# Attention logits as 64-row products on the two halves of the array

## The chip, the core and the metric

The kernel runs on one core of one Trainium2 chip. The core has TensorE (PE), which multiplies matrices; VectorE (DVE), ScalarE (ACT) and GpSimd (POOL), which work on vectors; SyncE (SP), which here only issues transfers; and 16 DMA engines that move data between HBM and SBUF, the on-chip memory of 128 partitions. PE writes its results into PSUM, a second memory of eight banks, and the other engines read them there. The metric is the time in microseconds of one execution on the device.

## What is computed

The reference is one layer of an encoder, applied to two requests with the same weights: a prompt of 1024 tokens (A in the kernel) and a sample of 512 tokens (B). After a normalisation one wide projection gives the columns of two branches. Branch A of the layer is a bidirectional mLSTM; branch B is a dilated window attention with three groups (window and dilation 128 and 1, 512 and 4, 2048 and 16) of 8 heads of 64 channels. The change touches only the attention, and of it only the logits:

```python
logits = jnp.einsum('bghnqe,bghnke->bghnqk', qr, kb) + bias[:, None]
logits = jnp.where(mask, logits, -jnp.inf)
mx = jnp.max(logits, axis=-1)
p = jnp.exp(logits - mx[..., None])
den = jnp.sum(p, axis=-1)
o = jnp.einsum('bghnqk,bghnke->bghnqe', p, vb)
```

The contraction of a logit runs over the 64 channels (e) of one head. The three groups are then mixed by their denominators, gated, projected, merged with the other branch and added to the input.

## The kernel before

Precise products of 32-bit numbers are made from two parts: each operand is split into a high and a low part in the type float32r, and three products (high by high, high by low, low by high) are added in one PSUM bank. The helper `mm3` (lines 211 to 213) is such a triple for the dense projections.

The program has stages. The prompt's long projections come first, then the mLSTM of A (`mlstm`), the attention of A (`attend`, `N.attend(A, ...)`), the mLSTM of B, the attention of B, and the last projections. From the first mLSTM on, the order of PE and of the SP queue is written out by hand (`manual_schedule`), and the order on DVE, ACT and POOL is a scheduler's. In the hand-written order a stage's own work alternates with steps of dense work of the same layer (`Fill`; a step is one `mm3` triple or so), a fixed number of steps for each stage (`STEPS`).

The attention works on pairs of heads. There are 12 units `u` for a request, group `g` and pair `pr` (`g, pr = divmod(u, 4)`), and each has `T.n` tiles of 128 queries: 8 for A, 4 for B, so 96 + 48 = 144 tiles. A tile is wide when the residue sub-sequence `S // dil` is longer than 128 (groups 0 and 1 of A, group 0 of B: 64 + 16 = 80 tiles) and reads 256 keys; the other 64 tiles are narrow and read 128 keys. For a tile there are four steps, in `stages`: `products` (the logits into the bank `lg`), `softmax` (DVE adds the bias and takes the maximum, line 1386, then ACT takes the exponential, line 1390), `turn` (PE transposes the weights into `pt`, line 1397, and ACT or DVE copies them out, lines 1400 and 1402) and `output` (PE multiplies by the values into `o`, lines 1411 and 1418, and ACT copies, lines 1414 and 1420). `att_round` runs one round for each tile: `products` of this tile, `softmax` of the one before, `turn` of the one before that, a helping of dense steps (`fill(1)`), and then `output` of the tile three rounds back. So on PE a round reads: `lg`, `pt`, dense, `o`, and the next round's `lg` follows directly on `o`.

How `products` uses the array differs between the two kinds of tile. Queries and keys lie in HBM in `T.aqk`, 128 rows for a pair: 64 channels of the first head, then 64 of the second, once for the high and once for the low part.

- Wide: the query operand of one head holds its high part in 64 rows and its low part in the other 64; the key operand of that head holds the same part of the keys twice, in both halves. One product with the high keys and one with the low keys, each over all 128 rows, then give all four combinations: 2 products for a head, 4 for a tile, each of 256 columns (line 1372).
- Narrow: the key operand is block diagonal: 128 columns with the first head's rows and zeros below, then 128 columns with zeros above and the second head's rows. One `mm3` of 128 rows and 256 columns serves both heads: 3 products for a tile. The zeros are set by memsets on POOL (line 1312), once for each buffer.

`att_load` queues the transfers for these layouts; `tick` issues some of the queue (SP) in each round. For a wide unit they are 4 for the queries and 8 for the keys, of 64 rows each, and for a narrow unit 1 and 4.

The tiles of PSUM in the attention are `lg`, `pt` and `o`, two buffers each, six banks together; two more are the dense projections'.

Of the kernel before, what the change touches and what calls it, by code (L numbers as in the profile page):

```python
# [22 lines left out]
F32 = mybir.dt.float32  # L23
# [6 lines left out]
P = 128  # L30
D = 1024
KT = D // P
BLK = 512
# [150 lines left out]
class Net:  # L184
    def __init__(self, tc, a):
        self.tc, self.nc, self.a = tc, tc.nc, a
        self.clock = self.lag = 0
        self.pending, self.owner = [], {}
        self.defer, self.mixed, self.rows = False, set(), {}
        self.queued, self.pace = [], 1  # L190
        self.side = self.nc.sync
        self.lows = None
        self.scans, self.state, self.held, self.sum = [], [], [], None
        self.low_part = None
        self.retired = []
        self.narrow, self.acc, self.direct = {}, [None, None], {}


    def pool(self, stack, name, bufs, side, space=None):
# [1068 lines left out]
    def att_load(self, T, u):  # L1268

        nc = self.nc
        g, pr = divmod(u, 4)
        S, n, dil = T.S, T.n, min(DILS[g], T.n)
        wide = S // dil > P
        A, B = slice(0, 64), slice(64, P)
        half = lambda x, i: x[:, i % 2 * 2 * S:(i % 2 + 1) * 2 * S]  # L1280
        if S == BLK:
            if u == 0:
                self.qs, self.avs = self.take("Q0"), self.take("X1", F32)
            q, v = half(self.qs, u), half(self.avs, u // 2)
            keys = lambda: [x for z in [self.take(f"V{u % 2}a")] for x in (z[:, :2 * S], z[:, 2 * S:])]
        else:
            if pr % 2 == 0:
                self.avs = self.take(f"K{u // 2 % 2}", F32)
            q, v = self.take(f"Q{u % 2}"), self.avs
            keys = lambda: [self.take(f"V{u % 2}{x}") for x in "ab"]  # L1290
        q = q.rearrange("p (a s) -> p a s", a=2)
        v = v.rearrange("p (n c) -> p n c", c=256)
        qd, kd = T.aqk[:, u], T.aqk[:, u + 12]
        if wide:
            kk = [x.rearrange("p (h s) -> p h s", h=2) for x in keys()]
            for hh, rows in enumerate((A, B)):
                self.queue(("att", u), ("aqk", S, u), q[rows, hh].bitcast(F32), qd[0, rows])
                self.queue(("att", u), ("aqk", S, u), q[(B, A)[hh], hh].bitcast(F32), qd[1, rows])
                for to in (A, B):
                    for i in range(2):  # L1300
                        self.queue(("att", u), ("aqk", S, u + 12), kk[i][to, hh].bitcast(F32), kd[i, rows])
            k = [x[:, hh] for x in kk for hh in range(2)]
        else:
            new = (T, u % 2) not in self.narrow
            if new:
                self.narrow[T, u % 2] = [x.rearrange("p (n b s) -> p n b s", n=n, b=2) for x in keys()]
            k = self.narrow[T, u % 2]
            self.queue(("att", u), ("aqk", S, u), q.bitcast(F32), qd.rearrange("a p s -> p a s"))
            for side, rows in enumerate((A, B)):
                for i in range(2):  # L1310
                    if new:
                        nc.gpsimd.memset(k[i][rows, :, 1 - side].bitcast(F32), 0.0)
                    self.queue(("att", u), ("aqk", S, u + 12), k[i][rows, :, side].bitcast(F32), kd[i, rows].rearrange("p (n s) -> p n s", s=P))
        if pr % 2 == 0:
            c0 = 512 * g + 256 * (pr // 2)
            x = S // dil // P
            for r in range(dil):
                self.queue(("att", u), ("av", S), v[:, r * x:(r + 1) * x],
                           T.av[:, c0:c0 + 256].rearrange("(x p r) c -> r p x c", p=P, r=dil)[r])
        return [q[:, 0], q[:, 1]], k, v  # L1320

    def attention(self, T, u, qkv, bias, sb, ps):

        nc = self.nc
# [3 lines left out]
        wide = L > P  # L1328
# [30 lines left out]
        def stages(turned, qp, kp, kt, bt, dst, ends):  # L1359
# [4 lines left out]
            ts = {}  # L1364

            def products():
                lg = self.bank("lg")
                if wide:
                    ts["lg"] = [lg[:, 0], lg[:, 1]]
                    for hh in range(2):  # L1370
                        for z in (k[hh], k[2 + hh]):
                            nc.tensor.matmul(lg[:, hh], q[hh][:, qs], z.rearrange("p (n j) -> p n j", j=P)[:, pair],  # L1372
                                             start=z is k[hh], stop=z is not k[hh])
                else:
                    kk = [z[:, kt[0]].rearrange("p a j -> p (a j)") for z in k]
                    ts["lg"] = [lg[:, 0, :P], lg[:, 0, P:2 * P]]
                    self.mm3(lg[:, 0], (q[0][:, qs], q[1][:, qs]), kk, True, True)

            def softmax():
                ls = ts["ls"] = sb.tile([P, 2, W], F32, name="ls", bufs=3)  # L1380
# [48 lines left out]
    def attend(self, T, fill, steps, first, banks, outs, after=None, beside=None, at=()):  # L1429

        nc = self.nc
        self.lag = 3
        with ExitStack() as st:
            ps = self.pool(st, "at_ps" + T.name, 2, "right", PSUM)
            sb = self.pool(st, "at" + T.name, 2, "right")
            shape = {"lg": [P, 2, 256], "pt": [P, 4, P], "o": [P, 4, P]}
            make = lambda b: ps.tile(shape[b], F32, name=b, bufs=2)
            spare = {b: make(b) for b in banks}  # L1440
            self.bank = lambda b: spare.pop(b) if b in spare else make(b)
            self.ot = Rot(self, [sb.tile([P, OW], F32, name=f"ot{i}", bufs=1) for i in range(outs)])
            tables = self.pool(st, "bias" + T.name, 1, "right")
            bias = Rot(self, [tables.tile([P, BLK], F32, name=f"bias{i}", bufs=1) for i in range(4)])
            if T.n > 4:
                tables.tile([P, 2560], F32, name="apart", bufs=1)
            tiles = []
            fill.stage(steps, 12 * T.n)

            self.xo_end = fill.done + steps  # L1450

            def ready(u):
                nonlocal bias
                if u == 4 and T.n <= 4:
                    b = [x[F32] for x in bias.bufs]
                    bias = Rot(self, [b[i][:, c:c + 256].bitcast(F32R) for i in range(2) for c in (0, 256)])
                    self.xo_bufs.insert(0, ("stage", b[2:]))
                return self.attention(T, u, first if u == 0 else self.att_load(T, u), bias, sb, ps)

            coming = ready(0)  # L1460
            self.need(("table", 0))
            for i in range(12):
                now = coming
                for j, t in enumerate(now):
                    if j == 1:
                        if i < 11:
# [304 lines left out]
def body(tc, a):  # L1771
# [3 lines left out]
    with ExitStack() as st:  # L1775
# [145 lines left out]
        with ExitStack() as s1:  # L1921
# [35 lines left out]
            with ExitStack() as s2:  # L1957
# [11 lines left out]
                with ExitStack() as s3:  # L1969
                    N.gate_sums(B, N.pool(s3, "sums", 1, "right"))  # L1970
                    lanes = N.lanes(B, N.pool(s3, "lane2", 1, "right"), lambda: N.bank("o").rearrange("p a b -> p (a b)"), True)
                    N.attend(A, fill, STEPS[1], kept["qkv"], ("pt", "o", "lg"), 10, hold("head", lambda: N.ml_load(B, 0)),
                             lanes, range(44, 96, 8))
                    for _ in lanes:
                        pass
                    N.close()
# [16 lines left out]
            N.rows_in = [N.sraw[:, :BLK]] + [N.osb.tile([P, BLK], F32, name=f"ymr{i}") for i in range(2)]  # L1993
            N.xo_bufs = [(i, [N.osb.tile([P, BLK], F32, name=f"xo{i}{j}") for j in range(2)]) for i in range(2)]
            N.postw = None
            N.attend(B, fill, STEPS[3], kept["qkv"], ("lg", "o", "pt"), 7)
# [70 lines left out]
```

## Time and profile before

| | |
|---|---|
| median of 3 runs | 2236.23 us (2234.92 to 2236.70) |
| profiled execution | 2236.86 us, of which the span of the trace is 2235.1 us |
| PE, PE's weight loads, DVE, ACT, POOL busy | 99%, 87%, 68%, 50%, 32% of the span |
| attention of A | about 1310 to 1618 us after the start of the span |
| attention of B | about 1835 to 2088 us |

How it is read: each instruction on PE that multiplies has a load of its weights ahead of it (PEld in the trace), which may run beside the product before it. The duration of a product counts from when it is taken up until its result is complete, so the durations of successive products overlap; what a product costs in a full stream is the distance between its start and the next one's start. A row such as `128*128 128x256` reads: weights of 128 rows by 128 columns, a moving operand of 128 rows by 256 columns. A product of 32-bit type (the `o` of line 1418 and 1411) stands as two records.

### The profile page before, as it was taken

Reading aid. Unit: us, or ns where it says so; the run is one execution under the profiler, and the core shown is the slowest. Engines: PE = TensorE matmul, PEld = TensorE weight load, DVE = VectorE, ACT = ScalarE, POOL = GpSimd, SP = SyncE. Lnnn points to the kernel's source line nnn. Section 1 sums busy time; section 2 is a strip of 40 time slices with the busy share of each in tenths; the row PEclk is TensorE's granted clock in tenths of the full one; section 3 lists DMA queues with packets and bytes.
Section 4 is the critical chain, followed back from the end, with each engine's and each line's share of the span. In section 5 each row is a group of like instructions: output and inputs, shape, how many; then the busy total and the mean of one; then the engine's idle time right before and its main releaser. Section 6 shows DMA issues by size and latency. Waiting matters only on the chain.

```text
span 2235.1 us, 34988 instructions
## 1 busy us (share of the span) xinstructions
PE 2218.1 (99%) x11962; PEld 1939.6 (87%) x11962; DVE 1523.7 (68%) x2989; ACT 1120.3 (50%) x2394; POOL 715.7 (32%) x988
## 2 busy tenths in 40 slices
PE   9999999999999999999999999999999999999998
PEld 8999888888888888888888889989888888888887
DVE  7775667687776665558887765555689855665674
ACT  7332343344444343456776655656666644554332
POOL 1000423333333222236677620011165522221221
PEclk9999999999999999999999999999999999999999
DMA  3742444433323223385754779997678887776663
GB/s 124 192 115 81 174 155 165 165 141 113 113 105 112 85 85 122 114 279 173 236 186 157 191 200 247 260 250 210 208 242 289 259 261 236 236 255 201 232 233 113
DMA packets 217661, 408.81 MB, mean 183 GB/s; under 512 B 24938, under 2 KB 128042, under 8 KB 217483
## 3 DMA queue, kind: packets, MB, share of 16 engines
q1 hardware_dynamic: 187784, 298.51, 42.7%
q0 software_dynamic: 26096, 95.47, 13.7%
q10 hardware_dynamic: 3602, 12.59, 1.4%
q8 instruction: 95, 1.56, 0.3%
q14 instruction: 84, 0.68, 0.1%
HBM read 286.75 MB, written 119.73 MB: 182 GB/s over the span
## 4 chain that ended last, share of the span: by engine, by line
PE 94%; issue 2%; DMA 2%; DVE 1%; ACT 1%; POOL 0%; SPq 0%; DVEq 0%; POOLq 0%; ACTq 0%
PE d L213 14%; PE d L211 14%; PE d L212 14%; PE dense L211 12%; PE dense L213 12%; PE dense L212 12%; PE o L1418 3%; PE pt L1397 2%; PE lg L1372 2%; PE num L213 1%; PE num L211 1%; PE num L212 1%; PE a L1088 1%; PE kv L211 1%; PE kv L212 1%
## 5 line engine op out<-in xcount | busy, mean ns | idle before, releaser
L211 PE MATMUL dense<-H,wh 128*128 128x512 f32 x664 | 270.3, 407 | 0.0
L213 PE MATMUL dense<-H,wl 128*128 128x512 f32 x664 | 260.6, 392 | 0.0
L212 PE MATMUL dense<-H,wh 128*128 128x512 f32 x664 | 260.4, 392 | 0.0
L212 PE MATMUL d<-Hl,phla 128*128 128x512 f32 x608 | 236.5, 389 | 0.0
L213 PE MATMUL d<-Hh,phla 128*128 128x512 f32 x608 | 236.5, 389 | 0.0
L211 PE MATMUL d<-Hh,phla 128*128 128x512 f32 x608 | 236.5, 389 | 0.0
L280 DVE TENSOR_TENSOR wl<-wraw,wh 128x1024 fp32r<-128x1024 f32 (+1 forms) x121 | 150.0, 1240 | 72.8 <-ACT wh L274 72.5
L1386 DVE CUSTOM_DVE_ANT_0 ls<-lg,bias 128x256 f32<-128x256 f32 (+2 forms) x336 | 103.0, 332 | 116.5 <-PE lg L1372 55.4
L211 PE MATMUL d<-Hh,phlb 128*128 128x512 f32 x456 | 177.4, 389 | 0.0
L212 PE MATMUL d<-Hl,phlb 128*128 128x512 f32 x456 | 177.4, 389 | 0.0
L213 PE MATMUL d<-Hh,phlb 128*128 128x512 f32 x456 | 177.4, 389 | 0.0
L1390 ACT ACTIVATE ls<-ls,nm 128x128 f32<-128x128 f32 (+1 forms) x288 | 124.8, 435 | 92.7 <-DVE nm L1388 58.9
L274 ACT ACTIVATE wh<-wraw 128x1024 fp32r<-128x1024 f32 (+1 forms) x124 | 128.5, 1036 | 77.0 <-PE dense L212 26.1
L213 PEld LDWEIGHTS dense<-H,wl 128*128 128x128 f32 x664 | 124.7, 188 | 28.0
L695 POOL TENSOR_TENSOR psum_w<-pw_raw 128x512 f32<-128x512 f32 x38 | 58.5, 1540 | 278.4 <-DMA pw_raw<-w_in 259.6
L213 PE MATMUL d<-vhi,Hl 128*128 128x322 f32 x448 | 140.5, 314 | 0.5 <-DVE Hl L431 0.3
L211 PE MATMUL d<-vhi,Hh 128*128 128x322 f32 x448 | 140.3, 313 | 0.1
L212 PE MATMUL d<-vlo,Hh 128*128 128x322 f32 x448 | 139.6, 312 | 0.0
L212 PEld LDWEIGHTS dense<-H,wh 128*128 128x128 f32 x664 | 125.3, 189 | 14.3
L211 PEld LDWEIGHTS dense<-H,wh 128*128 128x128 f32 x664 | 125.1, 188 | 14.4
L213 PEld LDWEIGHTS d<-Hh,phla 128*128 128x128 f32 x608 | 114.2, 188 | 23.7
L211 PEld LDWEIGHTS d<-Hh,phla 128*128 128x128 f32 x608 | 114.2, 188 | 23.6
(574 smaller groups left out, 6105.0 us busy)
## 6 DMA issues: line engine op xcount, KB each, us to landing
pw_raw<-w_in SPq DMA_DIRECT2D x76, 512.0 KB, 4.1
wraw<-w_in SPq DMA_DIRECT2D x64, 512.0 KB, 4.6
aqk_a<-pwk SPq DMA_DIRECT2D x48, 512.0 KB, 3.5
aqk_b<-sw SPq DMA_DIRECT2D x48, 256.0 KB, 6.2
wraw<-w_pm POOLq DMA_DIRECT2D x24, 512.0 KB, 6.0
wraw<-w_out POOLq DMA_DIRECT2D x24, 512.0 KB, 3.9
wraw<-w_v POOLq DMA_DIRECT2D x22, 430.0 KB, 6.9
qk_a<-pwk SPq DMA_DIRECT2D x16, 512.0 KB, 2.7
```

Of the source, the lines that this page charges most:

```text
L211: nc.tensor.matmul(out, lh, rh, start=start, stop=False, **kw)
L212: nc.tensor.matmul(out, lh, rl, start=False, stop=False, **kw)
L213: nc.tensor.matmul(out, ll, rh, start=False, stop=stop, **kw)
L274: high = nc.scalar.activation(hi[:, :n], raw[:, :n], AF.Copy)
L280: low = (self.lows or nc.vector).tensor_sub(lo[:, :n], raw[:, :n], hi[:, :n].bitcast(F32))
L695: self.nc.gpsimd.tensor_add(s[:, 0], ws[1][:, 0], ws[1][:, 1])
L1088: nc.tensor.matmul(p[:, c - c0], kT[:, ct, c * P:(c + 1) * P], qT[:, ct, c * P:(c + 1) * P], start=ct == 0, stop=ct == 1)
L1372: nc.tensor.matmul(lg[:, hh], q[hh][:, qs], z.rearrange("p (n j) -> p n j", j=P)[:, pair], start=z is k[hh], stop=z is not k[hh])
L1386: nc.vector.tensor_tensor_reduce(out=ls[rows, hh], in0=ts["lg"][hh][rows, of], in1=bt[rows, hh, by], scale=1.0, scalar=NEG, op0=OP.add, op ...
L1390: self.held = self.held[-3:] + [nc.scalar.activation(ls[:, hh], ls[:, hh], AF.Exp, bias=nm[:, hh:hh + 1], accum_out=ot[:, 128 + hh:129 + hh])]
L1397: nc.tensor.transpose(pp[:, hh * nk + x], ts["ls"][:, hh, x * P:(x + 1) * P], self.ident)
L1418: nc.tensor.matmul(po[:, hh * 64:hh * 64 + 64], pt[:, hh * nk + x], vh(kt[x], hh), start=x == 0, stop=x == nk - 1)
```

## The change

All tiles use the same layout now. Queries and keys are loaded as they lie in HBM, 128 rows for the pair, the high and the low part beside each other: 2 transfers for the queries and 2 for the keys of a unit, each of 128 rows. The duplicates of the wide keys, the block diagonal with its memsets and the attribute `narrow` are gone; `V0b` and `V1b` hold no keys any more.

A logit product takes only the 64 rows of one head: rows 0 to 63 (`late`) for the first head, rows 64 to 127 (`early`) for the second. For each of the three combinations (high by high, high by low, low by high) the first head's product is followed by the second head's, so that the two halves of the array are used in turn. The fourth combination (low by low), which the wide tiles had, is no longer computed. A tile has 6 products, of 256 columns when wide and of 128 when narrow. In the built program they carry the tile size 64 by 128 and the positions row 0 and row 64; everything around them (`o` before, `pt` after) has 128 by 128.

The two heads write into two banks, `lg0` and `lg1`, two buffers each. To stay at six banks, `pt` and `o` have one buffer each. The constants of the stages, the rounds and the number of dense steps are as before.

```diff
-        qd, kd = T.aqk[:, u], T.aqk[:, u + 12]
-        if wide:
-            kk = [x.rearrange("p (h s) -> p h s", h=2) for x in keys()]
-            for hh, rows in enumerate((A, B)):
-                self.queue(("att", u), ("aqk", S, u), q[rows, hh].bitcast(F32), qd[0, rows])
-                self.queue(("att", u), ("aqk", S, u), q[(B, A)[hh], hh].bitcast(F32), qd[1, rows])
-                for to in (A, B):
-                    for i in range(2):
-                        self.queue(("att", u), ("aqk", S, u + 12), kk[i][to, hh].bitcast(F32), kd[i, rows])
...
-            for side, rows in enumerate((A, B)):
-                for i in range(2):
-                    if new:
-                        nc.gpsimd.memset(k[i][rows, :, 1 - side].bitcast(F32), 0.0)
-                    self.queue(("att", u), ("aqk", S, u + 12), k[i][rows, :, side].bitcast(F32), kd[i, rows].rearrange("p (n s) -> p n s", s=P))
+        for x, y in ((q, u), (k, u + 12)):
+            for i in range(2):
+                self.queue(("att", u), ("aqk", S, y), x[:, i].bitcast(F32), T.aqk[i, y])
...
             def products():
-                lg = self.bank("lg")
-                if wide:
-                    ts["lg"] = [lg[:, 0], lg[:, 1]]
-                    for hh in range(2):
-                        for z in (k[hh], k[2 + hh]):
-                            nc.tensor.matmul(lg[:, hh], q[hh][:, qs], z.rearrange("p (n j) -> p n j", j=P)[:, pair],
-                                             start=z is k[hh], stop=z is not k[hh])
-                else:
-                    kk = [z[:, kt[0]].rearrange("p a j -> p (a j)") for z in k]
-                    ts["lg"] = [lg[:, 0, :P], lg[:, 0, P:2 * P]]
-                    self.mm3(lg[:, 0], (q[0][:, qs], q[1][:, qs]), kk, True, True)
+                lg = ts["lg"] = [self.bank(f"lg{hh}") for hh in range(2)]
+                for i, (x, y) in enumerate(((0, 0), (0, 1), (1, 0))):
+                    for hh, rows in enumerate((late, early)):
+                        z = k[rows, y].rearrange("p (n j) -> p n j", j=P)[:, pair]
+                        nc.tensor.matmul(lg[hh][:, :z.shape[1] * P], q[rows, x, qs], z, start=i == 0, stop=i == 2)
...
-            shape = {"lg": [P, 2, 256], "pt": [P, 4, P], "o": [P, 4, P]}
-            make = lambda b: ps.tile(shape[b], F32, name=b, bufs=2)
+            make = lambda b: ps.tile([P, 4, P], F32, name=b, bufs=1) if b[0] != "l" else ps.tile([P, BLK], F32, name=b, bufs=2)
```

More of the change, by code (lines that the diff above doesn't have):

```diff
@@ L195, in __init__ @@
         self.retired = []
-        self.narrow, self.acc, self.direct = {}, [None, None], {}
+        self.acc, self.direct = [None, None], {}
     def pool(self, stack, name, bufs, side, space=None):
@@ L1277, in att_load @@
         S, n, dil = T.S, T.n, min(DILS[g], T.n)
-        wide = S // dil > P
-        A, B = slice(0, 64), slice(64, P)
         half = lambda x, i: x[:, i % 2 * 2 * S:(i % 2 + 1) * 2 * S]
@@ L1283, in att_load @@
                 self.qs, self.avs = self.take("Q0"), self.take("X1", F32)
-            q, v = half(self.qs, u), half(self.avs, u // 2)
-            keys = lambda: [x for z in [self.take(f"V{u % 2}a")] for x in (z[:, :2 * S], z[:, 2 * S:])]
+            q, v, k = half(self.qs, u), half(self.avs, u // 2), self.take(f"V{u % 2}a")[:, :2 * S]
         else:
@@ L1288, in att_load @@
                 self.avs = self.take(f"K{u // 2 % 2}", F32)
-            q, v = self.take(f"Q{u % 2}"), self.avs
-            keys = lambda: [self.take(f"V{u % 2}{x}") for x in "ab"]
-        q = q.rearrange("p (a s) -> p a s", a=2)
+            q, v, k = self.take(f"Q{u % 2}"), self.avs, self.take(f"V{u % 2}a")
+        q, k = (x.rearrange("p (a s) -> p a s", a=2) for x in (q, k))
         v = v.rearrange("p (n c) -> p n c", c=256)
-        qd, kd = T.aqk[:, u], T.aqk[:, u + 12]
-        if wide:
-            kk = [x.rearrange("p (h s) -> p h s", h=2) for x in keys()]
-            for hh, rows in enumerate((A, B)):
-                self.queue(("att", u), ("aqk", S, u), q[rows, hh].bitcast(F32), qd[0, rows])
-                self.queue(("att", u), ("aqk", S, u), q[(B, A)[hh], hh].bitcast(F32), qd[1, rows])
-                for to in (A, B):
-                    for i in range(2):
-                        self.queue(("att", u), ("aqk", S, u + 12), kk[i][to, hh].bitcast(F32), kd[i, rows])
-            k = [x[:, hh] for x in kk for hh in range(2)]
-        else:
-            new = (T, u % 2) not in self.narrow
-            if new:
-                self.narrow[T, u % 2] = [x.rearrange("p (n b s) -> p n b s", n=n, b=2) for x in keys()]
-            k = self.narrow[T, u % 2]
-            self.queue(("att", u), ("aqk", S, u), q.bitcast(F32), qd.rearrange("a p s -> p a s"))
-            for side, rows in enumerate((A, B)):
-                for i in range(2):
-                    if new:
-                        nc.gpsimd.memset(k[i][rows, :, 1 - side].bitcast(F32), 0.0)
-                    self.queue(("att", u), ("aqk", S, u + 12), k[i][rows, :, side].bitcast(F32), kd[i, rows].rearrange("p (n s) -> p n s", s=P))
+        for x, y in ((q, u), (k, u + 12)):
+            for i in range(2):
+                self.queue(("att", u), ("aqk", S, y), x[:, i].bitcast(F32), T.aqk[i, y])
         if pr % 2 == 0:
@@ L1319, in att_load @@
                            T.av[:, c0:c0 + 256].rearrange("(x p r) c -> r p x c", p=P, r=dil)[r])
-        return [q[:, 0], q[:, 1]], k, v
+        return q, k, v
     def attention(self, T, u, qkv, bias, sb, ps):
@@ L1366, in products @@
             def products():
-                lg = self.bank("lg")
-                if wide:
-                    ts["lg"] = [lg[:, 0], lg[:, 1]]
-                    for hh in range(2):
-                        for z in (k[hh], k[2 + hh]):
-                            nc.tensor.matmul(lg[:, hh], q[hh][:, qs], z.rearrange("p (n j) -> p n j", j=P)[:, pair],
-                                             start=z is k[hh], stop=z is not k[hh])
-                else:
-                    kk = [z[:, kt[0]].rearrange("p a j -> p (a j)") for z in k]
-                    ts["lg"] = [lg[:, 0, :P], lg[:, 0, P:2 * P]]
-                    self.mm3(lg[:, 0], (q[0][:, qs], q[1][:, qs]), kk, True, True)
+                lg = ts["lg"] = [self.bank(f"lg{hh}") for hh in range(2)]
[3 more added lines that the diff above has]
+                        nc.tensor.matmul(lg[hh][:, :z.shape[1] * P], q[rows, x, qs], z, start=i == 0, stop=i == 2)
             def softmax():
@@ L1971, in body @@
                     lanes = N.lanes(B, N.pool(s3, "lane2", 1, "right"), lambda: N.bank("o").rearrange("p a b -> p (a b)"), True)
-                    N.attend(A, fill, STEPS[1], kept["qkv"], ("pt", "o", "lg"), 10, hold("head", lambda: N.ml_load(B, 0)),
+                    N.attend(A, fill, STEPS[1], kept["qkv"], ("pt", "o", "lg0", "lg1"), 10, hold("head", lambda: N.ml_load(B, 0)),
                              lanes, range(44, 96, 8))
@@ L1995, in body @@
             N.postw = None
-            N.attend(B, fill, STEPS[3], kept["qkv"], ("lg", "o", "pt"), 7)
+            N.attend(B, fill, STEPS[3], kept["qkv"], ("lg0", "lg1", "o", "pt"), 7)
             end = N.pool(s1, "end", 1, "right")
```

## The prediction

> **What bounds the kernel now.** I read the page first: busy time, the slices, the chain that ended last.
>
> ```profile
> span 2235.1 us, 34988 instructions
> PE 2218.1 (99%) x11962; PEld 1939.6 (87%) x11962; DVE 1523.7 (68%) x2989; ACT 1120.3 (50%) x2394; POOL 715.7 (32%) x988
> PE 94%; issue 2%; DMA 2%; DVE 1%; ACT 1%; POOL 0%; SPq 0%; DVEq 0%; POOLq 0%; ACTq 0%
> ```
>
> PE has nearly no gap and is 94% of the chain. So what the change adds to PE's stream or takes from it goes one to one into the time, and work saved on DVE, POOL or SP is worth only what it takes from PE's waits. The profiled execution took 2236.86 us, 0.6 above the median of the runs; sums below are made against it.
>
> The groups of instructions, shapes kept apart, count the logits: all 320 wide products have line 1372 (96 + 96 + 64 + 64), the narrow triples begin at line 211 (32 + 32). That is 80 wide tiles of 4 products and 64 narrow tiles of 3.
>
> ```profile
> L1372 PE MATMUL lg<-V1a,Q 128*128 128x256 f32 x96 | 25.4, 319 | 0.0
> L1372 PE MATMUL lg<-V0a,Q 128*128 128x256 f32 x96 | 24.4, 310 | 0.0
> L1372 PE MATMUL lg<-V1b,Q 128*128 128x256 f32 x64 | 17.0, 287 | 0.1
> L1372 PE MATMUL lg<-V0b,Q 128*128 128x256 f32 x64 | 16.8, 283 | 0.6 <-DMA og_a<-ot 0.6
> L211 PE MATMUL lg<-V0a,Q 128*128 128x256 f32 x32 | 11.7, 366 | 0.0
> L211 PE MATMUL lg<-V1a,Q 128*128 128x256 f32 x32 | 11.7, 366 | 0.0
> ```
>
> What a tile costs is read from starts in the timeline, first a wide tile, then a narrow one.
>
> ```profile
> 1501.78 0.36 PE L1372 MATMUL lg<-V1a,Q 128*128 128x256 f32 x1
> 1501.98 0.28 PE L1372 MATMUL lg<-V1b,Q 128*128 128x256 f32 x1
> 1501.98 0.19 PEld L1372 LDWEIGHTS lg<-V1a,Q 128*128 128x128 f32 x1
> 1502.10 0.28 PE L1372 MATMUL lg<-V1a,Q 128*128 128x256 f32 x1
> 1502.21 0.28 PE L1372 MATMUL lg<-V1b,Q 128*128 128x256 f32 x1
> 1502.33 0.60 PE L1397 MATMUL pt<-ident,ls 128*128 128x128 f32 x4
> ...
> 1519.19 1.00 PE L1418 MATMUL o<-K,pts 128*128 128x64 f32 x8
> 1520.00 0.36 PE L211 MATMUL lg<-V0a,Q 128*128 128x256 f32 x1
> 1520.21 0.28 PE L212 MATMUL lg<-V0b,Q 128*128 128x256 f32 x1
> 1520.33 0.28 PE L213 MATMUL lg<-V0a,Q 128*128 128x256 f32 x1
> 1520.45 0.60 PE L1397 MATMUL pt<-ident,ls 128*128 128x128 f32 x4
> ```
>
> A 256-column product costs 0.12 in the stream; from the first logit to `pt` a wide tile takes 0.55 and a narrow one 0.45. The eight `o` records are 0.10 apart (0.81 over 8), so the last of them starts 0.09 ahead of the first logit. The third row shows a load starting together with the product before it: loads are hidden.
>
> **The price of changing the array's shape.** The logits will be 64 by 128 between neighbours of 128 by 128, 144 times in and out. The trace has that change in the gate computation, among A's narrow tiles:
>
> ```profile
> 1575.33 0.28 PE L1024 MATMUL o<-ident,l_q 128*128 128x128 f32 x1
> 1575.53 0.14 PEld L1025 LDWEIGHTS o<-ident,l_one 64*128 64x128 f32 x1
> 1575.53 0.27 PE L1025 MATMUL o<-ident,l_one 64*128 64x64 f32 x1
> 1575.74 0.19 PEld L211 LDWEIGHTS lg<-V0a,Q 128*128 128x128 f32 x1
> 1575.74 0.38 PE L211 MATMUL lg<-V0a,Q 128*128 128x256 f32 x1
> 1575.84 0.19 PEld L212 LDWEIGHTS lg<-V0b,Q 128*128 128x128 f32 x1
> 1575.96 0.28 PE L212 MATMUL lg<-V0b,Q 128*128 128x256 f32 x1
> 1575.96 0.19 PEld L213 LDWEIGHTS lg<-V0a,Q 128*128 128x128 f32 x1
> ```
>
> At both edges of the 64-row product the next load doesn't start with the product before it but 0.20 and 0.21 later, after that product has streamed and about 0.10 more. And the load is then bare: line 211 is taken up at 1575.74 and the next product follows 0.22 later, 0.11 of load and 0.11 of streaming. Loads of 128 columns follow each other at 0.10 to 0.11 (1575.74, 1575.84).
>
> The tile after, from the start T of the last `o` record. Wide: load at T+0.20, first pair streams to T+0.42; if the two halves run at once, each further pair costs one product, 0.12, so the third pair starts at T+0.54 and `pt`'s load 0.21 later (0.11 streaming, 0.10 more) at T+0.75; that load is a short one (0.14 as at line 1025 against 0.19, so 0.06 bare), `pt` at T+0.81. Before: 0.09 + 0.55 = T+0.64. So +0.17, and 80 x 0.17 = +13.6. Narrow: the first pair's load at T+0.20; the second and third loads follow at 0.11, the products are ready at T+0.42 and T+0.53, the last streams 0.05 (half of 256 columns' 0.11), `pt`'s load at T+0.69 and `pt` at T+0.75. Before: 0.09 + 0.45 = T+0.54. So +0.21, and 64 x 0.21 = +13.4. Together +27. Without the change of shape (0.10 and a bare load, twice, some 0.3 a tile) the same sum would be a gain.
>
> **Whether the halves run at once** no row shows; in before no two products lie on different halves. One end is a pair for the price of one product, the other two full prices: 3 more products a tile, 3 x 0.12 x 80 + 3 x 0.11 x 64 = +50. Against the overlap speaks the spacing of loads above, 0.10 to 0.11 at the closest; for it, that a pair shares neither rows nor bank, and that PE already works on a load and a product together. I take the overlap, and keep +50 for the range. The Trainium skill, "TensorE: Matmul & The Clock Gate", section Measured speedup vs the span model, prices a pack of tiles at one product and about 4 ns for each further one; by it alone, with no price for changing shape, the wide tile would take some 0.36 of logits instead of 0.55, and the change would save. The trace's line 1025 says that the edges cost more than that saves. No run here shows the overlap itself.
>
> **128 columns in float32r** don't occur before either. Low end: half of the 256-column product, hidden under the load's 0.11, as taken. High end: the 32-bit product of the same width.
>
> ```profile
> 1504.52 0.61 PE L1411 MATMUL o<-K,pts 128*128 128x128 f32 x4
> 1504.89 0.36 PE L1372 MATMUL lg<-V1a,Q 128*128 128x256 f32 x1
> ```
>
> Two products (four records) in 0.37 are 0.18 each, 0.07 over 0.11: 3 x 0.07 x 64 = +13 with the overlap, twice that without. I take the low end: the type is the logits' own, and the 32-bit product needs two records.
>
> **Transfers.** Bytes fall where PE did wait. In the attention of A:
>
> ```profile
> 1300.00:1475.00 175.00, 173.70 (x1177) 166.71 (x1176) 99.49 (x388) 104.99 (x340) 10.56 (x22) 1.00 0.96 245
> 1475.00:1500.00 25.00, 22.84 (x137) 21.69 (x136) 13.96 (x62) 14.01 (x48) 5.98 (x8) 0.86 1.04 272
> ...
> 1490.79 0.92 ACT L274 ACTIVATE wh<-wraw 128x860 fp32r<-128x860 f32 x1 [5.25 <-DMA wraw<-w_v]
> ...
> 1493.57 1.19 PE L1397 MATMUL pt<-ident,ls 128*128 128x128 f32 x4 [2.07 <-ACT ls L1390]
> ...
> Q<-aqk_a SPq DMA_DIRECT2D x32, 256.0 KB, 6.2
> V0a<-aqk_a SPq DMA_DIRECT2D x20, 256.0 KB, 7.5
> ```
>
> The second-last column of the windows is the DMA engines' share, about full. A late weight holds ACT for 5.25, the exponentials behind it are late, PE waits 2.16 (25.00 - 22.84), and after the wait the granted clock is low: 0.86 over those 25 us, a loss of at most 0.14 x 25 = 3.5. Between them 2.2 to 5.7 at stake. A wide unit of A had 4 query and 8 key transfers of 256 KB and has 4 of 512 KB: 1 MB of 3 less, 8 MB over 8 units, about 19% of the 43 MB that 245 GB/s move in the first window's 175 us. SP issues 12 transfers a wide unit before and 4 after, a narrow one 5 and 4, and what queues behind them (the `og` stores) moves up. The late weight should come earlier: I take -4, between 0 (another transfer takes the freed time) and -5.7. POOL's memsets go; they delayed nothing on PE's chain, so 0.
>
> **`pt` and `o` with one buffer.** A round is some 3 us (logits at 1501.78 and, of the next tile, at 1504.89). `o` must now be copied within one round instead of two. ACT copies in order, so what holds ACT holds PE:
>
> ```profile
> 1465.29 0.26 ACT L1420 ACTIVATE ot<-o 128x128 f32<-128x128 f32 x1
> 1470.72 0.51 ACT L1390 ACTIVATE ls<-ls,nm 128x256 f32<-128x256 f32 x1 [5.16 <-issue]
> ...
> 1843.18 1.06 ACT L274 ACTIVATE X<-wraw 128x1024 fp32r<-128x1024 f32 x1 [4.63 <-DMA wraw<-w_pm]
> ```
>
> There ACT stood 5 us, about two rounds; with one buffer PE would wait 2 to 3 at each (5 less a round of 3, or a little more). Three such stands (with the one at 1490) would make at most +9; the rounds get longer and two of the three lie in the saturated stretch, so I take +1, between 0 and +9. Queued behind a waiting `o` on PE is the next tile's `lg`, and behind that `softmax` on DVE.
>
> Sum: 13.6 + 13.4 - 4 + 1 = +24; 2236.9 + 24 = 2261.
>
> **Rivals.**
> - Halves one after the other: 2261 + 50 = 2311. For it: the load spacing. Against: disjoint rows and banks.
> - Narrow products at the 32-bit price: 2261 + 13 = 2274 with the overlap, 2311 + 27 = 2338 without.
> - Faster: the gaps at line 1025 are waits for its inputs and not the change of shape, and the overlap holds. Then wide tiles save one product, 80 x 0.12 = -9.6, narrow ones 3 x 0.01 x 64 = -2: 2236.9 - 9.6 - 2 - 4 + 1 = 2222. It decides where the two edges cost under (9.6 + 2 + 3) / 144 = 0.10 a tile. Against it: the second edge, whose logits of line 211 had their operands long before, shows the same 0.21. The Trainium skill, "TensorEngine Tiling (Array Packing)", Key Properties, says that a change of tiling mode drains the engine; the trace agrees.
> - An edge between the two halves as well: each of the 6 products pays load, streaming and 0.10: 0.32 wide, 0.26 narrow; wide T+0.20 + 1.92 + 0.06 = T+2.18 (+1.54), narrow T+1.82 (+1.28): 80 x 1.54 + 64 x 1.28 - 3 = +202, 2439. In the trace an edge stands only where the shape changes, and the halves share one shape.
>
> **Numbers.** Overlap 0.42, with the dear narrow products 0.12; one after the other 0.24, with the dear ones 0.06; faster 0.11; edges everywhere 0.05. The likeliest gives 2261, its own range 2252 to 2272 (transfers -5.7 to 0, one buffer 0 to +9, edges 0.03 a tile either way). The range 2250 to 2340 takes in the first four, 0.84. This kernel's runs tell 0.2%, 4.5 us, from no change: faster 0.11, same 0.03, slower 0.86.
>
> **What will show it.** Right: six `lg` products of 64 rows a tile, the first load 0.20 after the last `o` record and `pt`'s load 0.15 to 0.21 after the last logit; pairs starting nearly together and pairs 0.11 to 0.12 apart; from first logit to `pt` about 0.6; the DMA share between 1310 and 1500 well under 0.96 and no long wait of `pt`. Wrong: starts evenly 0.11 apart (one after the other), loads under the preceding product at the edges (faster), 32-bit-like records of 0.18 in the narrow tiles, or new waits of `o` for ACT.

## The result

The changed kernel takes 2258.83 us (median; 2258.36 to 2260.20) against 2236.47 us for the kernel before beside it: a ratio of 1.0102, 95% interval 1.0084 to 1.0119, 22.4 us slower. 2261 was predicted, with a range of 2250 to 2340.

The page of the changed kernel, the lines that answer to those of before:

```profile
span 2258.2 us, 35358 instructions
PE 2243.1 (99%) x12314; PEld 1938.9 (86%) x12314; DVE 1523.7 (67%) x2989; ACT 1122.6 (50%) x2394; POOL 700.6 (31%) x972
PE 96%; DVE 1%; ACT 1%; issue 1%; DMA 1%; POOL 0%; DVEq 0%; SPq 0%; POOLq 0%; ACTq 0%
```

PE is still the bound, and is 25 us busier. DVE and ACT are as busy as before (ACT 2 us more). The timeline of PE in the changed kernel, a wide tile and then a narrow one (the rows merge equal instructions; the first number is the start of the first of them):

```profile
1504.06 1.00 PE L1390 MATMUL o<-K,pts 128*128 128x64 f32 x8
1504.99 0.63 PE L1349 MATMUL lg<-V1a,Q 64*128 64x256 f32 x6
1505.55 0.66 PE L1369 MATMUL pt<-ident,ls 128*128 128x128 f32 x4
1505.96 0.44 PE L211 MATMUL dense<-wh,H 128*128 128x430 f32 x1
...
1563.01 0.55 PE L1390 MATMUL o<-K,pts 128*128 128x64 f32 x4
1563.49 0.55 PE L1349 MATMUL lg<-V1a,Q 64*128 64x128 f32 x6
1563.97 0.44 PE L1369 MATMUL pt<-ident,ls 128*128 128x128 f32 x2
1564.16 0.48 PE L211 MATMUL dense<-H,X 128*128 128x512 f32 x1
```

And the same stretches of the kernel before, from its timeline, without the rows of single logits:

```profile
1500.97 1.00 PE L1418 MATMUL o<-K,pts 128*128 128x64 f32 x8
...
1502.69 0.44 PE L211 MATMUL dense<-wh,H 128*128 128x430 f32 x1
...
1584.66 0.55 PE L1418 MATMUL o<-K,pts 128*128 128x64 f32 x4
...
1585.60 0.48 PE L211 MATMUL dense<-H,wh 128*128 128x512 f32 x1
```

From the first `o` to the dense product after `pt` the wide tile took 1.72 us and takes 1.90 (+0.18); the narrow one took 0.94 and takes 1.15 (+0.21). The loss is at the two borders of the logits: eight `o` records to the first logit were 0.81 and are 0.93 (1504.06 to 1504.99), four `pt` records were 0.36 and are 0.41 (1505.55 to 1505.96). The logits themselves, from their first start to `pt`, take 0.56, as much as the four 128-row products did (0.55), since inside that 0.56 stands the wait for the last logits to run out (the drain) ahead of `pt`. The two products of a pair do start together: the 30 ns from 1504.98 to 1505.01 hold both of the first pair,

```profile
1504.99 0.39 PE L1349 MATMUL lg<-V1a,Q 64*128 64x256 f32 x2
```

four are under way by 1505.23 and all six by 1505.345. These are the signs that the prediction named.

On PE the attention's products (`o`, `lg`, `pt`) stand in blocks between dense products. The time from a block's first start to the next dense product, summed over all blocks of a trace and without PE's idle time, leaves waits aside. It is 210.3 us in the changed kernel and 182.3 in the 128-row kernel without the stall that is measured further down (low keys loaded once): 28.0 more.

Where the loss lands in the span is read from the first and last start of the logits of each request, first before, then after (the columns are minimum, median and maximum duration in ns and the first and last start in us):

```profile
L1372 PE MATMUL lg<-V0a,Q x64: 277/283/366, 1309.6 to 1487.4; 128*128 128x256 f32 x64
L213 PE MATMUL lg<-V1a,Q x16: 279/281/283, 1542.3 to 1608.1; 128*128 128x256 f32 x16
L1372 PE MATMUL lg<-V0a,Q x32: 277/283/365, 1816.9 to 1877.6; 128*128 128x256 f32 x32
L213 PE MATMUL lg<-V1a,Q x16: 281/285/285, 1928.7 to 2068.8; 128*128 128x256 f32 x16
```

```profile
L1349 PE MATMUL lg<-V0a,Q x288: 268/279/384, 1308.1 to 1596.0; 64*128 64x256 f32 x96, 64*128 64x128 f32 x48
L1349 PE MATMUL lg<-V1a,Q x288: 268/279/384, 1335.2 to 1620.4; 64*128 64x256 f32 x96, 64*128 64x128 f32 x48
L1349 PE MATMUL lg<-V0a,Q x144: 270/274/383, 1831.1 to 2070.5; 64*128 64x128 f32 x96, 64*128 64x256 f32 x48
L1349 PE MATMUL lg<-V1a,Q x144: 270/276/383, 1852.3 to 2091.8; 64*128 64x128 f32 x96, 64*128 64x256 f32 x48
```

(B's first logit stands at 1816.9, ahead of the 1835 of the table of times before.) From the first logit to the last, A's attention went from 298.5 us to 312.3 (+13.8), B's from 251.9 to 260.7 (+8.8). By the tiles A should have grown by 64 x 0.18 + 32 x 0.21 = 18.2 and B by 16 x 0.18 + 32 x 0.21 = 9.6. So 4.4 us came back in A, on balance; the stall is gone there:

```profile
1300.00:1475.00 175.00, 174.41 (x1219) 156.88 (x1218) 96.64 (x375) 101.66 (x324) 10.19 (x21) 1.00 0.65 206
1475.00:1500.00 25.00, 25.00 (x181) 22.71 (x181) 14.39 (x61) 15.79 (x54) 2.19 (x4) 1.00 0.69 203
```

The DMA engines' share fell from 0.96 and 1.04 to 0.65 and 0.69, PE is busy for all of the 25 us in which it had waited 2.16, and the granted clock there is 1.00 instead of 0.86.

### The profile page after: what moved, and what is told of

Read it like the earlier page. It is cut to its first block, busy times and chain, and to the rows that moved or that the text cites. A ratio compares the mean times of both kernels' runs of the same rounds, so it can differ in the third digit from the quotient of the medians.

```text
span 2258.2 us, 35358 instructions
## 1 busy us (share of the span) xinstructions
PE 2243.1 (99%) x12314; PEld 1938.9 (86%) x12314; DVE 1523.7 (67%) x2989; ACT 1122.6 (50%) x2394; POOL 700.6 (31%) x972
## 4 chain that ended last, share of the span: by engine, by line
PE 96%; DVE 1%; ACT 1%; issue 1%; DMA 1%; POOL 0%; DVEq 0%; SPq 0%; POOLq 0%; ACTq 0%
PE d L213 13%; PE d L211 13%; PE d L212 13%; PE dense L211 12%; PE dense L213 12%; PE dense L212 12%; PE lg L1349 3%; PE o L1390 3%; PE pt L1369 3%; PE num L211 1%; PE num L213 1%; PE num L212 1%; PE a L1088 1%; PE kv L211 1%; PE kv L212 1%; PE kv L213 1%
```

## The experiments

The kernel before ran beside each of them, at 2235.7 to 2236.4 us.

**Do the halves run at once?** The prediction took the overlap on trust. One kernel puts both heads on one half, one puts a fourth pair in, one changes the order.

```diff
-                    for hh, rows in enumerate((late, early)):
+                    for hh, rows in enumerate((late, late)):
```

> The changed kernel with both heads' products on rows 0 to 63: the second head's six operands are taken from the first head's rows, so its logits are those of the first head and the output is not the reference's. The same products, edges, banks and transfers; only the halves are no longer two. Theory (the halves run at once, a pair for the price of one product): without a second half the pairs fall apart, 3 x 0.117 x 80 + 3 x 0.11 x 64 = 49 us over the changed kernel, about 2308. Rival (the order of the head-by-head kernel made no difference because the products run one after the other anyway): 2259.

Measured: 2306.42 us, 47.6 over the changed kernel. Its logits, and below them those of the changed kernel, each from the groups of instructions (the two groups of 256 columns):

```profile
L1349 PE MATMUL lg<-V1a,Q 64*128 64x256 f32 x240 | 38.9, 295 | 0.0
L1349 PE MATMUL lg<-V0a,Q 64*128 64x256 f32 x240 | 38.8, 295 | 0.0
```

```profile
L1349 PE MATMUL lg<-V1a,Q 64*128 64x256 f32 x240 | 24.8, 312 | 0.0
L1349 PE MATMUL lg<-V0a,Q 64*128 64x256 f32 x240 | 24.8, 312 | 0.0
```

The same 240 products keep PE busy for 38.9 us on one half and for 24.8 on two, and a wide tile's six take 0.90 us from the first start to `pt` (1503.06 to 1503.96) instead of 0.56. The overlap is real, and the price of doing without it is the predicted one (49).

```diff
-                for i, (x, y) in enumerate(((0, 0), (0, 1), (1, 0))):
+                for i, (x, y) in enumerate(((0, 0), (0, 1), (1, 0), (1, 1))):
...
-                        nc.tensor.matmul(lg[hh][:, :z.shape[1] * P], q[rows, x, qs], z, start=i == 0, stop=i == 2)
+                        nc.tensor.matmul(lg[hh][:, :z.shape[1] * P], q[rows, x, qs], z, start=i == 0, stop=i == 3)
```

> The changed kernel with a fourth pair of products a tile (low by low, which it leaves out). It measures the price of one more pair of 64-row products inside the same two edges. Theory (a pair costs one product, 0.117 wide and 0.11 narrow): 80 x 0.117 + 64 x 0.11 = 16 us, 2275. Rival (one after the other): 33 us, 2292.

Measured: 2276.83 us, 18.0 over the changed kernel; over 144 tiles that is 0.125 us a tile, about the price of one product (0.11). The two products one after the other would have been about double.

```diff
-                for i, (x, y) in enumerate(((0, 0), (0, 1), (1, 0))):
-                    for hh, rows in enumerate((late, early)):
+                for hh, rows in enumerate((late, early)):
+                    for i, (x, y) in enumerate(((0, 0), (0, 1), (1, 0))):
```

> The changed kernel with its six logit products in another order: the three of the first head, then the three of the second, everything else the same. Theory (the halves run at once, a pair for one product): a product can then overlap only with the next one in order, so of three pairs only the middle one is left, five steps instead of three, 2 x 0.117 x 80 + 2 x 0.11 x 64 = 33 us over the changed kernel, about 2292 us; 2309 if even the middle pair falls apart. Rival (the products run one after the other in the changed kernel already): the order makes no difference, 2259.

Measured: 2260.54 us; the order makes no difference. That is the rival's number, but not by the rival's mechanism, as the kernel on one half shows. The theory had a wrong detail: that a product starts only after the one ahead of it in the order has started. A narrow slit of the timeline at the first logits of one tile, 25 ns wide, first with the three products of each head in a row, then with all on one half:

```profile
1376.90 0.39 PE L1349 MATMUL lg<-V0a,Q 64*128 64x256 f32 x2
```

```profile
1503.06 0.38 PE L1349 MATMUL lg<-V0a,Q 64*128 64x256 f32 x1
```

In the first kernel two products are under way in this stretch, in the second only one. Since products on one half don't overlap, the other one must be the second head's first, the fourth in the order: it has passed the second and the third. (The rows don't name the head, so this is concluded, not read.)

**What does a change of shape cost by itself?** The kernel before, with one 64-row product a tile put ahead of the logits.

```diff
                 lg = self.bank("lg")
+                z = k[0] if wide else k[0][:, kt[0]].rearrange("p a j -> p (a j)")
+                nc.tensor.matmul(lg[:, 0], q[0][late, qs], z[late, :256], start=True, stop=True)
```

> The kernel before with one more product a tile: 64 rows by 256 columns of the first head, into the bank lg ahead of the real logits, which overwrite it. It measures a change of shape by itself. Theory: the load starts 0.20 after the last o record, the product streams after a bare load of 0.11, and the next full product again has its load 0.21 later and bare; 0.46 us a tile, 144 x 0.46 = 66 us, about 2302. Rival (a change of shape is free and the load hidden): one product of 0.117 a tile, 17 us, 2253.

Measured: 2295.21 us, 59 over before. Its timeline at a wide tile:

```profile
1382.64 0.18 PEld L1369 LDWEIGHTS lg<-V0a,Q 64*128 64x128 f32 x1
1382.65 0.38 PE L1369 MATMUL lg<-V0a,Q 64*128 64x256 f32 x1
1382.95 0.19 PEld L1374 LDWEIGHTS lg<-V0a,Q 128*128 128x128 f32 x1
1382.96 0.38 PE L1374 MATMUL lg<-V0a,Q 128*128 128x256 f32 x1
1383.06 0.19 PEld L1374 LDWEIGHTS lg<-V0b,Q 128*128 128x128 f32 x1
1383.18 0.28 PE L1374 MATMUL lg<-V0b,Q 128*128 128x256 f32 x1
```

The 64-row product is taken up at 1382.65, the next load 0.30 later (0.11 bare load, 0.11 streaming, 0.08 to 0.10 more), and the second full product starts 0.22 after the first (1382.96 to 1383.18), whose load is bare too. One small product costs 0.45 a tile here: the blocks take 247.4 us, 65.1 over the 182.3 of the 128-row kernel without the stall, and 65.1 / 144 = 0.45. The time grew by 59 and not by 65 or 66, since the stall of before (some 5 us) is gone in this kernel too: PE is busy without a gap from 1300 to 1500.

```profile
1300.00:1475.00 175.00, 175.00 (x1089) 158.94 (x1087) 86.73 (x327) 95.37 (x302) 10.54 (x22) 1.00 0.86 224
1475.00:1500.00 25.00, 25.00 (x158) 23.04 (x157) 15.41 (x73) 13.22 (x49) 0.55 (x1) 1.00 0.84 219
```

**Half the borders.** The products of two tiles together, every second round.

```diff
+                    if j % 2 == 0:
+                        self.pair = self.two = now[j:j + 2]
...
+        i = len(tiles) - 1
         for age, stage in ((0, 0), (1, 1), (2, 2), (None, None), (3, 3)):
...
+            elif stage < 2:
+                if i % 2 == stage and tiles[i - stage] is not None:
+                    for t in self.two if stage else self.pair:
+                        t[stage]()
```

> The changed kernel with the products of two tiles issued together in every second round, and their softmaxes together in the round after; the same products, transfers and banks, but half as many changes of the array's shape (72 in and out instead of 144). Theory (each edge pair costs 0.29 us: 0.17 + 0.117 in a wide tile): 72 x 0.29 = 21 us less than the changed kernel, about 2238. Rival (64-row products are dear in themselves, or the single buffers of pt and o are): no gain, 2256 to 2260.

Measured: 2243.95 us, 14.9 less than the changed kernel; only the softmaxes moved along with the products. On PE the gain is the forecast one: the blocks take 188.9 us instead of 210.3, 21.4 less. Part of it goes again into PE's waits, for copies of `o`, which has one buffer and shorter rounds now: five waits of 2.6 us in total, and one of 1.1. The remaining 2.8 are not explained.

```profile
PE o L1390 <- ACT ot L1386: 2.6, 5, 1.2
PE o L1390 <- ACT ot L1392: 1.1, 1, 1.1
```

**Wide tiles alone.** Narrow tiles stay as in the kernel before, with their transfers and memsets.

```diff
...
+                if not wide:
+                    kk = [z[:, kt[0]].rearrange("p a j -> p (a j)") for z in k]
+                    ts["lg"] = [lg[0][:, :P], lg[0][:, P:2 * P]]
+                    self.mm3(lg[0][:, :256], (q[:, 0, qs], q[:, 1, qs]), kk, True, True)
+                    return
```

> The change for the wide tiles alone: narrow tiles keep the block-diagonal keys and the one triple of 128 rows and 256 columns (into the bank lg0), wide tiles take 64-row products; pt and o have one buffer. Theory: the narrow tiles' 64 x 0.218 = 14 us go, 2245. If the narrow tiles were the whole loss it would be about 2236 or less; if they cost nothing, 2259.

Measured: 2251.04 us, 7.8 less than the changed kernel, not 14. The blocks take 196.7 us, 13.6 less, so the narrow tiles did cost what was forecast. A's logits span 1309.2 to 1615.9 and B's 1826.7 to 2081.9, 5.6 and 5.5 us less than in the changed kernel; two waits for copies of `o`, 1.1 us in total, are new. The profiled execution, the shortest of its four, is 10.4 us under the changed kernel's, which is the longest of its four. What makes the medians differ by 7.8 alone is not explained.

**One buffer for `pt` and `o`**, in the kernel before.

```diff
-            make = lambda b: ps.tile(shape[b], F32, name=b, bufs=2)
+            make = lambda b: ps.tile(shape[b], F32, name=b, bufs=2 if b == "lg" else 1)
```

> The kernel before, in which only pt and o get one buffer instead of two. Theory: ACT's stands of 5 us reach PE, but seldom; 0 to 9 us over before, most likely 2238. Rival (the single buffers make a good part of the loss): 2245 to 2258, with long waits of PE for ACT's copies of o and pt.

Measured: 2243.37 us (2236.07 to 2250.35), 7.1 over before, interval of the ratio 1.0018 to 1.0038: inside the 0 to 9, well over its likeliest 2238, and just short of the rival's 2245. In the short rounds of the kernel before the second buffer is worth 4 to 8 us. In the profiled execution, the longest of its twelve (2250.35), PE waits for the copies as the prediction drew it, some 3 us at a time:

```profile
PE o L1418 <- ACT ot L1414: 3.3, 1, 3.3
PE pt L1397 <- DVE pts L1402: 2.9, 1, 2.9
PE o L1418 <- ACT ot L1420: 2.6, 2, 2.2
```

**Did the saved transfers end the stall?** One kernel gives the changed kernel its 8 MB back:

```diff
+        if S // dil > P and S > BLK:
+            z = self.take(f"V{u % 2}b")[:, :2 * S].rearrange("p (a s) -> p a s", a=2)
+            for i in range(2):
+                for rows in (slice(0, 64), slice(64, P)):
+                    self.queue(("att", u), ("aqk", S, u + 12), z[rows, i].bitcast(F32), T.aqk[i, u + 12, rows])
```

> The changed kernel, which for each wide unit of the prompt also loads the keys a second time into the buffers V0b and V1b, in four transfers of 64 rows as before did; nothing reads them. That gives back the 8 MB that the change saves. Theory (the saved transfers end the late weight, worth 4 us): 2263, with ACT waiting for a weight and the pt transposes after it somewhere between 1400 and 1520 us. Rival (the stall went for another reason, such as longer rounds): 2259, no stall.

Measured: 2258.59 us. No stall came back; the rival holds. By itself this leaves a doubt, since the DMA engines' share rose only to 0.79 and 0.84. But the kernel with the small product above has all the transfers of before, and longer rounds, and no stall either: longer rounds are enough to end it. The next kernel takes transfers from the kernel before and leaves its rounds short:

```diff
...
-                for to in (A, B):
-                    for i in range(2):
-                        self.queue(("att", u), ("aqk", S, u + 12), kk[i][to, hh].bitcast(F32), kd[i, rows])
+                for i in range(2):
+                    if new:
+                        nc.gpsimd.memset(kk[i][(B, A)[hh], hh].bitcast(F32), 0.0)
+                    self.queue(("att", u), ("aqk", S, u + 12), kk[i][rows, hh].bitcast(F32), kd[i, rows])
```

> The kernel before, in which the wide keys are loaded once: each head's keys only into its own 64 rows, the other 64 rows hold zeros set once on POOL. The products of queries' low parts with keys fall out of the wide logits (they meet the zeros), so the output is not the reference's; shapes and number of products are as before. It takes away the 8 MB and 64 transfers alone, with the short rounds of before. Theory (the transfers held up the late weight): the stall at 1490 us goes, 4 to 5 us less than before, about 2232. Rival (only longer rounds end the stall): 2236 and the stall stays, or comes elsewhere.

Measured: 2232.88 us, ratio 0.9983 (0.9974 to 0.9992). The stall is gone, with the rounds as short as before, and A's logits span 1311.0 to 1602.6, 291.6 us instead of 298.5. (The profiled execution is the longest of its eleven, 2235.36, and loses 5.4 of these 6.9 us outside A's logits, 2.8 of them between the two attentions, where the code is that of before.)

```profile
1300.00:1475.00 175.00, 175.00 (x1186) 168.22 (x1185) 102.04 (x396) 106.52 (x342) 12.49 (x26) 1.00 0.82 214
1475.00:1500.00 25.00, 25.00 (x174) 24.49 (x173) 15.38 (x64) 16.71 (x59) 5.39 (x7) 1.00 0.88 239
```

So fewer transfers are enough as well. Either of two changes ends the stall, longer rounds or fewer transfers, and the changed kernel has both.

**Versions that the findings ask for.** The low keys alone loaded once, which keeps the changed kernel's three combinations in 128-row products:

```diff
...
+                other = (B, A)[hh]
+                if new:
+                    nc.gpsimd.memset(kk[1][other, hh].bitcast(F32), 0.0)
+                for to, i in ((rows, 0), (other, 0), (rows, 1)):
+                    self.queue(("att", u), ("aqk", S, u + 12), kk[i][to, hh].bitcast(F32), kd[i, rows])
```

> The kernel before, in which only the low part of the wide keys is loaded once: in its own 64 rows, with zeros in the other 64. The three combinations of the changed kernel remain (low by low falls out, as there), in 128-row products without any change of shape, with two buffers of pt and o; 6 key transfers of a wide unit instead of 8, 4 MB less in the prompt's attention. Theory (transfers alone end the stall, the edges and single buffers cost): the stall of 5 us goes or shrinks, 2231 to 2235, under both kernels. Rival (half of the saved bytes isn't enough): 2236.

Measured: 2232.75 us, ratio 0.9985 (0.9976 to 0.9994). PE has no wait between 1475 and 1500, and A's logits span 292.4 us.

And 64-row products where they save one (wide tiles), four tiles to a pair of borders, with the wide units' transfers of the changed kernel:

```diff
...
+                if not turned:
+                    both[:] = [self.bank(f"lg{hh}") for hh in range(2)]
+                lg = ts["lg"] = [x[:, turned * 256:turned * 256 + 256] for x in both]
...
+        if now is not None:
+            for t in [now] if not now[4] else self.four if i % 4 == 0 else []:
+                t[0]()
+        if last is not None and (not last[4] or i % 4 == 1):
+            last[1]()
+        if now is not None and now[4] and i % 4:
+            now[1]()
...
```

> A kernel that the theory asks for: wide tiles take 64-row products, those of four tiles issued together at the head of each group of four rounds (two tiles share a bank of each head), so an edge pair serves four tiles; narrow tiles keep the block diagonal; transfers as in the changed kernel for wide units; pt and o with one buffer. Theory: a wide tile saves 0.117 - 0.29 / 4 = 0.045 against before, 80 x 0.045 = 3.6 us, and the late weight's 4 us go: 2229, under both kernels. Rival (bunching the softmaxes or the single buffers bring new waits): 2236 or more.

Measured: 2233.02 us, ratio 0.9986 (0.9977 to 0.9994). Its timeline shows 24 products in 1.62 us from the first logit to `pt`, 0.41 a tile with the drain ahead of `pt`, against 0.55 before:

```profile
1385.70 1.00 PE L1416 MATMUL o<-K,pts 128*128 128x64 f32 x8
1386.63 1.69 PE L1375 MATMUL lg<-V1a,Q 64*128 64x256 f32 x24
1388.25 0.66 PE L1395 MATMUL pt<-ident,ls 128*128 128x128 f32 x4
```

Both are some 3 us under the kernel before and 26 under the changed one. The first gets its 3 us with 128-row products, from the transfers alone. The 64-row products of the second do save time on PE, 177.6 us of blocks against 182.3, 4.7 less (3.6 was forecast). But PE waits for copies of `o` in it, as one buffer makes it do, and the first has no such wait:

```profile
PE o L1416 <- ACT ot L1412: 1.9, 3, 1.0
PE o L1416 <- ACT ot L1418: 1.6, 2, 1.2
```

These 3.5 us take most of the saving back. No run shows 64-row products making this kernel faster than 128-row products with fewer transfers make it.

## Why the prediction was right, step by step

- **The borders** (+13.6 for the wide, +13.4 for the narrow tiles): right. 0.17 and 0.21 a tile were drawn from the gate computation's 64-row transpose; the timeline shows 0.18 and 0.21, and the blocks grew by 28.0, where 27 was forecast. Half the borders take 21.4 off the blocks, narrow tiles as before take 13.6 off, and the kernel with one small product a tile pays the borders alone. The rival that ends faster, that the gaps at line 1025 were waits for inputs, falls with that kernel: its small product reads the same queries and keys as the logits beside it, and pays 0.45 a tile over all 144 tiles.
- **The overlap**, taken between +0 and +50: right, and now shown; one half costs +47.6, a fourth pair +18.0. It was a choice, without a row for it, when it was made. That pairs fall apart, and borders inside the pairs, are out.
- **128 columns in float32r**, taken at the low end: right. From the first logit to `pt` a narrow tile takes 0.48, three pairs at the loads' 0.11 and the drain ahead of `pt`.
- **The transfers** (-4): too small, and the cause was only half of it. A got 4.4 back on balance, beside 1.8 of new waits (next point), so some 6 came back. That the balance looks like the forecast is luck. The step read: fewer bytes, so the late weight comes earlier. The transfers given back changed nothing (2258.59), since longer rounds alone are enough, as the kernel with the small product shows with all the transfers of before.
- **One buffer for `pt` and `o`** (+1, up to +9): near enough for the changed kernel, whose only waits of this kind are those of the gate computation, all in A's attention, 1.8 us in total:

```profile
PE o L948 <- ACT ot L1392: 0.6, 1, 0.6
PE o L981 <- ACT ot L1392: 0.4, 1, 0.4
PE o L1002 <- ACT ot L1392: 0.4, 1, 0.4
PE o L1024 <- ACT ot L1392: 0.4, 1, 0.4
```

In the short rounds of the kernel before it is 7. That the longer rounds are what keeps it small in the changed kernel fits the waits of 3.7 us with half the borders, but no run gives the changed kernel the second buffers.
- **The sum**: 18.2 + 9.6 of borders less 4.4 and 0.8 make 22.6 in the two attentions; the 0.8 in B is not explained. Between them 1.9 us were lost and ahead of them 1.5 gained (1309.6 to 1308.1); the code there is the same, and other kernels begin the attention between 1307.3 and 1311.0, so these stay unexplained scatter of builds and runs. That makes 23 between the two profiled executions; the medians differ by 22.4, and 24 was forecast. The prediction's narrow range, 2252 to 2272, does not follow from the terms that it names: added up, they give about 2254 to 2277. The result lies in either.

## What to carry to other kernels

Small products on two halves of the array do run at once (0.56 us for six, 0.90 on one half), but changing the array's shape exposes a drain and a load on both sides, some 0.3 us together here (21.4 us for 72 pairs of borders), so a packed group must save more than that. Put several tiles' packed products behind each other before packing at all, and count what the packing takes elsewhere: here the banks for it were taken from `pt` and `o`, and the waits that this brought cost most of what four tiles together had saved. Look in the trace of the kernel at hand for an instruction that already has the new shape: one 64-row transpose gave the price of a tile to within 0.01 us. And when a stall disappears with a change, give the suspected cause back before crediting it: here slower rounds alone had ended it too.

## What the runs showed of the hardware that was not expected

The two halves take their products from the order independently: with the first head's three products ahead of the second head's three, the fourth started within 25 ns of the first, and 2260.54 us against 2258.83 is no loss that stands out of the noise. In which order the products alternate made no difference here.

Nearly equal rates of transfer kept the DMA engines busy for unequal shares: 0.96 at 245 GB/s before, and 0.79 at 242 GB/s in the changed kernel with its 8 MB given back; 0.82 at 214 GB/s with the wide keys loaded once (its row is above), and 0.68 at the same 214 with four tiles together. In the changed kernel and in the one with four tiles a wide unit's transfers have 128 rows and 512 KB, where those of before and of the keys loaded once have 64 rows and 256 KB (the 8 MB given back came in such small ones too). The shares go with that, but rows and size were not tried by themselves. The rows of the two kernels with 128-row transfers, 8 MB given back and four tiles together:

```profile
1300.00:1475.00 175.00, 174.54 (x1223) 157.05 (x1222) 96.77 (x375) 102.15 (x328) 9.37 (x17) 1.00 0.79 242
1300.00:1475.00 175.00, 172.58 (x1290) 161.65 (x1289) 103.65 (x402) 106.83 (x348) 10.90 (x23) 1.00 0.68 214
```
